# Split weight tiles with longer rows, and pools that begin on multiples of 512 bytes, in a hybrid decoder layer

## The chip, the cores and the metric

One core of one Trainium2 chip runs one layer of a decoder. The metric is device time in microseconds, the median of three runs. A profile of one execution stands beside the times; it also says which clock TensorE was granted.

## What is computed

x has 256 tokens of 2048 channels, all in fp32. The layer is

```
h      = rms_norm(x, mix_norm)
proj   = h @ w_in
mixers = dilated attention, RG-LRU, sliding GQA, SSD   (from slices of proj)
merged = sum over 4 branches of sigmoid(gate_b) * (mixer_b @ w_branch[b])
x      = x + merged @ w_out
gate, up = split(rms_norm(x, ffn_norm) @ w_ffn_in)
x      = x + (silu(gate) * up) @ w_ffn_out
```

The weights are some 354 MB, each used once for the 256 tokens. Most of the work is these five products with big weights.

## The kernel before, in words

**One helper does all the big products.** `stream` (L123 to L156) works off one chunk of at most 512 columns of a weight. For every two row blocks of 128 (one `kg`, KG = 2) it takes a raw fp32 tile `wr`, makes its high part `wh` on ScalarE (a copy into fp32r, L143) and its low part `wl = wr - wh` on VectorE (L145), and multiplies. A tile `wr` comes by one DMA for four row blocks. The product of two fp32 numbers is made of three fp32r passes: activations high by `wh` (L151), high by `wl` (L152), low by `wh` (L153). The stationary operand of each pass is a 128 x 128 slice of the transposed activations (512 bytes in each partition); the moving operand is one row of `wh` or `wl`: 512 columns, 2048 bytes in each partition. For each row block there are two token blocks and three passes, so six matmuls, and twelve for each `kg`. A pass is 128 x 512 wide in all chunks but the first four, which are 384 or 396 wide.

**Buffers.** `wh` and `wl` (pool `wp`, tags `whi` and `wlo`) have four buffers each of [128, 2, 512] fp32r, 4096 bytes in each partition, and lie one behind the other; `wr` has three of 8192 bytes behind them. The stationary operands are `hT_hi`, `hT_lo` (then `x2T_hi`, `x2T_lo` in the same place, pool `actp`), `br_hi`, `br_lo` for the branch projections, `gT_hi`, `gT_lo` for the last product, all on the left side of SBUF, and `mT_hi`, `mT_lo` for the output projection (`ps_o`), on the right side.

**Where they lie modulo 512.** SBUF is handed out from 16512 on (left) and down to 229376 less 32 (right). The pool `const` comes first on the left; with `bsb` it is 4640 + 1536 = 6176 bytes long, so `wp` begins at 22688, which is 160 modulo 512. All buffers behind it are multiples of 512 long, so every row of `wh` and `wl` that is 512 wide, and every slice of `hT`, `x2T`, `br` and `gT`, begins at 160 modulo 512. On the right, `x2` (16384 bytes) begins at 212960, which is 480 modulo 512, and the slices of `mT_hi` and `mT_lo` below it begin at 480 too.

**Order.** All instructions are written out in Python; a scheduler orders them by priority, and the weight stream (DMA, `wh`, `wl`) has the highest. Between the chunks' matmuls small pieces of the mixers are let in by `pump` (transposes and attention matmuls in plain fp32, on the same TensorE queue). The chunks come in this order: 5 of the SSD branch (`ps_ssm`), 3 of the LRU branch (`ps_lru`), 16 of attention (`ps_att`), 16 gate chunks (`ps_g`) with 16 branch projections (`ps_b`) between them, 4 of the output projection (`ps_o`), 22 of the FFN (`ps_fg`, `ps_fu` in turn), 4 of its last product (`ps_fo`).

**The bias vector.** `bias_vector` (L261) runs once, early: one small matmul, a copy into `bsb` (L265) and a DMA to DRAM (L266). `staged` (L322) copies a chunk's results from PSUM into tiles `stg` of the tag `tok`, which has three buffers in the pool `aq`.

Of the kernel before, what the change touches and what calls it, by code (L numbers as in the profile page):

```python
# [18 lines left out]
P = 128  # L19
# [7 lines left out]
KG = 2  # L27
# [8 lines left out]
G0 = M0 + 768 + 1280 + 12  # L36

UNITS = [("c", 0), ("c", 1)] + [("a", h) for h in range(6)]
SSM_W = (384, 384, 384, 396, 512)


def unit_slices():
    """128-column slices of the attention branches: (unit, kind, index, start)."""
    out = []
    for u, (kind, i) in enumerate(UNITS):
        if kind == "c":
            out += [(u, "q", g, C0 + (3 * i + g) * DH) for g in range(3)]
            out += [(u, "k", 0, C0 + 768 + i * DH), (u, "v", 0, C0 + 1024 + i * DH)]
        else:
            out += [(u, s, g, ((si * 3 + g) * 6 + i) * DH) for si, s in enumerate("qkv") for g in range(3)]  # L50
    return out
# [5 lines left out]


def chunk_plan():
    """Column slices (start, width) of w_in in the order in which they are worked off."""  # L60
    z, xbc, dt = M0, M0 + 768, M0 + 768 + 1280
    plan = [("ssm", j, [(xbc + 384 * j, 384)]) for j in range(3)]
    plan += [("ssm", 3, [(xbc + 1152, 128), (z, 256), (dt, 12)]), ("ssm", 4, [(z + 256, 512)])]
    plan += [("lru", j, [(L0 + 512 * j, 512)]) for j in range(3)]
    plan += [("att", j, [(c, DH) for _, _, _, c in SL[4 * j : 4 * j + 4]]) for j in range(len(SL) // 4)]
    return plan


def group_size(kc, first=False):
    """Row blocks of a weight that one transfer carries."""  # L70
    return KG if first or kc % KD else KD


# [1 line left out]
def hybrid(ctx, tc, a):  # L75
    nc = tc.nc
    V, A, G, PE = nc.vector, nc.scalar, nc.gpsimd, nc.tensor

    const = ctx.enter_context(tc.tile_pool(name="const", bufs=1))
    wp = ctx.enter_context(tc.tile_pool(name="wp", bufs=4))  # L80
    actp = ctx.enter_context(tc.tile_pool(name="actp", bufs=1))
    psm = ctx.enter_context(tc.tile_pool(name="psm", bufs=2, space=PSUM))
    psx = ctx.enter_context(tc.tile_pool(name="psx", bufs=4, space=PSUM))
    dram = ctx.enter_context(tc.tile_pool(name="dram", bufs=1, space=DRAM))

    def ctile(shape, name, src=None, dt=F32):
        t = const.tile(shape, dt, name=name, tag=name)
        if src is not None:
            nc.sync.dma_start(t, src)
        return t  # L90
# [1 line left out]
    def mps(name):  # L92
        return psx.tile([P, 512], F32, name=name, tag="mps")

# [1 line left out]
    side = {"near": deque(), "far": deque()}  # L96

    def advance(queue):
# [24 lines left out]
    def stream(src, offset, kc, n, hi, lo, name, before=None, first=False):  # L123
        kd = group_size(kc, first)
        ps = psm.tile([P, T, 512], F32, name=f"ps_{name}", tag="psmain")
        for kg in range(kc // KG):
            if before is not None:
                before(kg)
            with tc.high_priority(offset=4000):
                if kg % (kd // KG) == 0:  # L130
                    if first:
                        raw = xp.tile([P, kd, n], F32, name=f"wr_{name}_{kg}", tag="wfirst", bufs=6)
                    else:
                        raw = wp.tile([P, kd, n], F32, name=f"wr_{name}_{kg}", tag="wraw", bufs=RAW, padded_shape=[P, KD, 512])
                    o = offset + kg * P * KG * n
                    nc.sync.dma_start(
                        raw,
                        bass.AP(tensor=src.tensor, offset=src.offset + o, ap=[[kd * n, P], [n, kd], [1, n]]),
                    )
                q = kg % (kd // KG) * KG  # L140
                rk = raw[:, q : q + KG]
                wh = wp.tile([P, KG, n], F32R, name=f"wh_{name}_{kg}", tag="whi")
                A.activation(wh, rk, AF.Copy)  # L143
                wl = wp.tile([P, KG, n], F32R, name=f"wl_{name}_{kg}", tag="wlo")
                V.tensor_tensor(wl, rk, wh.bitcast(F32), op=ALU.subtract)  # L145
            last = kg == kc // KG - 1
            for kk, t in [(kk, t) for t in range(T) for kk in range(KG)] if last else [(kk, t) for kk in range(KG) for t in range(T)]:
                k = kg * KG + kk
                xh, xl = hi[:, k, t * P : (t + 1) * P], lo[:, k, t * P : (t + 1) * P]
                o_ps = ps[:, t, :n]  # L150
                PE.matmul(o_ps, xh, wh[:, kk], start=(k == 0), stop=False)  # L151
                PE.matmul(o_ps, xh, wl[:, kk], start=False, stop=False)  # L152
                PE.matmul(o_ps, xl, wh[:, kk], start=False, stop=(k == kc - 1))  # L153
            if kg < kc // KG - 1:
                pump()
        return ps  # L156

# [1 line left out]
    with tc.high_priority(offset=4100):  # L159
        gmix = ctile([P, 16], "gmix", a["mix_norm"])  # L160
    actA_hi = actp.tile([P, 16, S], F32R, name="hT_hi", tag="actA_hi")
# [16 lines left out]
    V.memset(negh, -0.5)  # L178

    def rsqrt(out, ss, scale, eps, n):  # L180
        """out = (ss * scale + eps) ** -0.5 on [P, n]"""
        t = const.tile([P, n], F32, name="rsq_t", tag=f"rsq{n}", bufs=2)
        V.tensor_scalar(t, ss, scale, eps, op0=ALU.mult, op1=ALU.add)
        G.tensor_tensor(out, t, negh.to_broadcast([P, n]), op=ALU.pow)
# [37 lines left out]
    ps_first = [next_chunk("ssm", load_input), next_chunk("ssm", load_tokens)]  # L222
    head.close()

# [1 line left out]
    ident = ctile([P, P], "ident", a["ident"])  # L226
    tri = ctile([P, P], "tri", a["tri"])
    ones = ctile([P, P], "ones")
# [22 lines left out]
    V.tensor_scalar(lgb, lgb, 0.5, None, op0=ALU.mult)  # L251
    V.tensor_scalar(snorm, snorm, 0.5, None, op0=ALU.mult)

# [1 line left out]
    tabx = ctile([36, 24], "tabx")  # L255
    nc.sync.dma_start(tabx[0:32, :], a["rel_bias_table"])
    nc.sync.dma_start(tabx[32:36, :], a["group_neg"])
# [3 lines left out]
    def bias_vector():  # L261
        bps = mps("bias_ps")
        PE.matmul(bps[:24, :384], tabx, onehot, start=True, stop=True)
        bsb = ctile([24, 384], "bsb")
        V.tensor_copy(bsb, bps[:24, :384])  # L265
        nc.sync.dma_start(bvec, bsb)  # L266
        yield

    mix = ExitStack()
# [5 lines left out]
        br_lo[b] = pool.tile([P, 6, S], F32R, name=f"br_lo{b}", tag=f"br_lo{b}")  # L275

    def softplus(pool, x, n, name):
        """max(x, 0) + log1p(exp(-|x|)), the logarithm by its series in e / (2 + e)."""

        def st(s):  # L280
            return pool.tile([P, n], F32, name=f"{name}_{s}", tag=f"{name}_{s}", bufs=1)
# [15 lines left out]
        return pl  # L297

    def transpose4(blocks, name):
        """Up to four [128, 128] blocks, transposed into one bank."""  # L300
        ps = mps(name)
        for i, b in enumerate(blocks):
            PE.transpose(ps[:, i * P : (i + 1) * P], b, ident)
        return ps

    # =============== SSD and LRU branches ===============
    branch_operands(3)
    branch_operands(1)
    att1 = ExitStack()
# [10 lines left out]
                V.scalar_tensor_tensor(out[:, b], src[:, b, k : k + S], w[:, b, k : k + 1], out[:, b], op0=ALU.mult, op1=ALU.add)  # L320

    def staged(ps, n, name):  # L322
        """[tokens, n] of PSUM, normalised, as one SBUF tile for each token block."""
        out = []
        for t in range(T):
            stg = aq.tile([P, 512], F32, name=f"stg_{name}{t}", tag="tok", bufs=3)
            A.activation(stg[:, :n], ps[:, t, :n], AF.Copy, scale=r1[:, t : t + 1])
            out.append(stg)
        return out
# [6 lines left out]
            )  # L336
            yield

    # z and dt by token; x, B, C by channel
    zz = sp_.tile([P, T, BW], F32, name="zz", tag="zz")  # L340
    dtx = sp_.tile([P, T, 12], F32, name="dtx", tag="dtx")
    xbcT = sp_.tile([P, 10, S + 3], F32, name="xbcT", tag="xbcT")
# [188 lines left out]
    def lru_body():  # L531
# [40 lines left out]
                    )  # L572

        def decay(s2):
            """a and 1 - a^2 = tanh(-log a) (1 + a^2)"""
            for b in range(s2.start, s2.stop):
                A.activation(th[:, b], tr[:, b], AF.Tanh, scale=c4[:, b : b + 1], bias=c4[:, b : b + 1])
                A.activation(la[:, b], tr[:, b], AF.Exp, scale=nc4[:, b : b + 1], bias=nc4[:, b : b + 1])
# [29 lines left out]
        later(to_channels(staged(ps, 512, f"l{j}"), 4, lruT, 4 * j, f"l{j}"), "near", 1)  # L608
    later(lru_body(), "far", 3)

    # =============== attention branches ===============
    pools = {}
    att = ExitStack()
    unit = [{} for _ in UNITS]
# [12 lines left out]
        return unit[u][s]  # L627

    def qkv_chunk(ps, sl, name):
        """[tokens, slices] in PSUM -> q and k normalised and transposed to [dh, slice, tokens], v by token."""  # L630
        qk = [(i, x) for i, x in enumerate(sl) if x[1] != "v"]
        m = len(qk)
        toks = []
# [143 lines left out]
        later(qkv_chunk(next_chunk("att"), SL[4 * j : 4 * j + 4], f"t{j}"), "near")  # L777
        advance(side["near"])

    # =============== gates, branch projections, merge ===============  # L780
    order = (1, 3, 2, 0)
    gmp = pools["gate"]

# [36 lines left out]
                    G.tensor_tensor(mg[:, t], mg[:, t], gt[:, t], op=ALU.add)  # L820
        later(merged_channels(c, mg), "near", 2)

    # =============== output projection, residual, FFN norm ===============
    x2 = pools["res"].tile([P, T, D], F32, name="x2", tag="x2")
    nc.sync.dma_start(x2, a["x"].rearrange("(t p) d -> p t d", p=P))
    ss2 = ctile([P, T, 4], "ss2")
# [36 lines left out]
    hrr2 = ctile([P, T], "hrr2")  # L863
    V.tensor_tensor(hrr2, hr2, r2, op=ALU.mult)

    # =============== FFN ===============
    def gated_channels(j, sa):
        for q in range(2):
            tp = transpose4([sa[:, t, (2 * q + i) * P : (2 * q + i + 1) * P] for i in range(2) for t in range(T)], f"ftp{j}{q}")
# [28 lines left out]


def _blocks(w, slices, first=False):  # L900
    """[K, n] columns as contiguous [group, partition, k, n] blocks."""
    m = np.concatenate([w[:, o : o + n] for o, n in slices], axis=1)
    k, n = m.shape
    kd = group_size(k // P, first)
    return np.ascontiguousarray(m.reshape(k // P // kd, kd, P, n).transpose(0, 2, 1, 3)).reshape(-1)
# [21 lines left out]


def _cols(v, n):
    """[n*128] -> [128, n]"""  # L930
    return np.ascontiguousarray(np.asarray(v).reshape(n, P).T)


def _layout(i):
# [4 lines left out]
    parts = [_blocks(w_in, sl, (kind, j) == ("ssm", 0)) for kind, j, sl in chunk_plan()]  # L939
    parts += [_blocks(w_in, [(G0 + b * D + c * 512, 512)]) for c in range(4) for b in (1, 3, 2, 0)]  # L940
    onehot, neg = _bias_constants()
    conv = lambda w, b, n: np.ascontiguousarray(  # noqa: E731
        np.concatenate([np.asarray(w)[0], np.asarray(b)[0][None]], 0).reshape(5, n, P).transpose(2, 1, 0)
    )
    qa, qc = np.asarray(i["qk_norm_a"])[0], np.asarray(i["qk_norm_c"])[0]
# [43 lines left out]
```

## Time and profile before

| | |
|---|---|
| median of 3 runs | 1905.21 us (1904.8 to 1905.32) |
| span of the profiled execution (first to last instruction) | 1903.2 us |
| its time outside the span, by the median of the runs | 2.0 us |
| granted TensorE clock, mean | 1.000 of 2.4 GHz |
| PE busy | 1891.0 us (99%), 8714 matmul records |
| PEld (weight loads, beside PE) | 1577.9 us (83%) |
| DVE, ACT, POOL busy | 1081.3, 860.3, 178.5 us |
| DMA | 358.09 MB, mean 188 GB/s |
| chain that ended last | PE 98%, issue 2% |

A matmul's recorded duration runs on beyond the start of the next one, because matmuls are pipelined. What one costs in a row of them is the distance from its start to the next start, which the timeline shows to 10 ns; over a dozen of them the mean is good to 1 ns. The profiled execution's own time is not listed apart from the three runs, so it is taken as its span and the 2.0 us that lie around it.

### The profile page before, as it was taken

The page shows a single profiled execution, that of the slowest core. Times are in us where ns is not written, and L with a number is a line of the kernel's source. Part 1 is how long each engine was busy: PE and PEld are TensorE (multiplying, and loading weights), DVE is VectorE, ACT ScalarE, POOL GpSimd, SP SyncE. Part 2 cuts the span into 40 slices and gives each one's busy share as a digit, 9 for nine tenths or more (in the row PEclk, how much of TensorE's full clock was granted, in tenths as well). Part 3 has the DMA queues.
Part 4 walks back from the last instruction along what each step waited for, and adds up shares of the span by engine and source line. Part 5 has one row for each costly group of instructions (what it writes and reads, how often), then busy time and mean ns, then how long its engine had stood idle before and what let it go on. Part 6 is the DMA issues. An engine that isn't in the chain of part 4 may idle for free.

```text
span 1903.2 us, 21867 instructions
## 1 busy us (share of the span) xinstructions
PE 1891.0 (99%) x8714; PEld 1577.9 (83%) x8714; DVE 1081.3 (57%) x1234; ACT 860.3 (45%) x1052; POOL 178.5 (9%) x152
## 2 busy tenths in 40 slices
PE   8999999999999999999999999999999999999998
PEld 8988888888888888888888888888888888888887
DVE  6867886555555555555555555555555555544443
ACT  6645654444444444444444444444444444433332
POOL 0032322222220000100000100000000000000000
PEclk9999999999999999999999999999999999999999
DMA  8644454454544554555546545555555555555552
GB/s 294 203 154 171 162 210 170 163 185 177 185 171 169 199 213 163 211 186 191 209 166 221 188 177 178 197 181 195 187 190 193 184 198 180 196 187 201 209 209 101
DMA packets 64915, 358.09 MB, mean 188 GB/s; under 512 B 8049, under 2 KB 17581, under 8 KB 26925
## 3 DMA queue, kind: packets, MB, share of 16 engines
q1 hardware_dynamic: 64812, 356.70, 52.6%
q8 instruction: 68, 1.11, 0.2%
q14 instruction: 35, 0.28, 0.0%
HBM read 354.54 MB, written 2.13 MB: 187 GB/s over the span
## 4 chain that ended last, share of the span: by engine, by line
PE 98%; issue 2%; DVE 0%; POOL 0%; DVEq 0%; POOLq 0%
PE ps_att L151 6%; PE ps_att L153 6%; PE ps_att L152 6%; PE ps_g L151 6%; PE ps_g L153 6%; PE ps_g L152 6%; PE ps_fg L153 4%; PE ps_fg L151 4%; PE ps_fg L152 4%; PE ps_fo L151 4%; PE ps_fu L153 4%; PE ps_fu L152 4%; PE ps_fo L152 4%; PE ps_fo L153 4%; PE ps_fu L151 4%; PE ps_b L151 2%
## 5 line engine op out<-in xcount | busy, mean ns | idle before, releaser
L145 DVE TENSOR_TENSOR wl_g<-wr_g,wh_g 128x1024 fp32r<-128x1024 f32 x128 | 170.0, 1328 | 145.7 <-ACT wh_g L143 145.6
L143 ACT ACTIVATE wh_g<-wr_g 128x1024 fp32r<-128x1024 f32 x128 | 135.9, 1062 | 194.2 <-PE ps_g L153 118.6
L145 DVE TENSOR_TENSOR wl_att<-wr_att,wh_att 128x1024 fp32r<-128x1024 f32 x128 | 159.6, 1250 | 92.4 <-ACT wh_att L143 92.2
L143 ACT ACTIVATE wh_att<-wr_att 128x1024 fp32r<-128x1024 f32 x128 | 135.5, 1060 | 163.9 <-PE ps_att L153 145.2
L151 PE MATMUL ps_att<-wh_att,hT_hi 128*128 128x512 f32 x512 | 206.3, 403 | 0.0
L151 PE MATMUL ps_g<-wh_g,hT_hi 128*128 128x512 f32 x512 | 200.5, 392 | 0.0
L153 PE MATMUL ps_att<-wh_att,hT_lo 128*128 128x512 f32 x512 | 199.9, 391 | 0.0
L152 PE MATMUL ps_att<-wl_att,hT_hi 128*128 128x512 f32 x512 | 199.6, 390 | 0.0
L153 PE MATMUL ps_g<-wh_g,hT_lo 128*128 128x512 f32 x512 | 199.3, 389 | 0.0
L152 PE MATMUL ps_g<-wl_g,hT_hi 128*128 128x512 f32 x512 | 199.3, 389 | 0.0
L145 DVE TENSOR_TENSOR wl_fo<-wr_fo,wh_fo 128x1024 fp32r<-128x1024 f32 x88 | 107.9, 1226 | 124.7 <-ACT wh_fo L143 124.7
L145 DVE TENSOR_TENSOR wl_fu<-wr_fu,wh_fu 128x1024 fp32r<-128x1024 f32 x88 | 107.9, 1226 | 118.9 <-ACT wh_fu L143 118.9
L145 DVE TENSOR_TENSOR wl_fg<-wr_fg,wh_fg 128x1024 fp32r<-128x1024 f32 x88 | 107.8, 1225 | 106.9 <-ACT wh_fg L143 106.9
L143 ACT ACTIVATE wh_fo<-wr_fo 128x1024 fp32r<-128x1024 f32 x88 | 93.4, 1061 | 145.9 <-PE ps_fo L153 139.3
L143 ACT ACTIVATE wh_fg<-wr_fg 128x1024 fp32r<-128x1024 f32 x88 | 93.4, 1061 | 143.4 <-PE ps_fg L153 70.3
L143 ACT ACTIVATE wh_fu<-wr_fu 128x1024 fp32r<-128x1024 f32 x88 | 93.4, 1061 | 133.9 <-PE ps_fg L153 72.9
L151 PE MATMUL ps_fg<-wh_fg,x2T_hi 128*128 128x512 f32 x352 | 139.1, 395 | 0.0
L153 PE MATMUL ps_fg<-wh_fg,x2T_lo 128*128 128x512 f32 x352 | 137.3, 390 | 0.0
L151 PE MATMUL ps_fo<-wh_fo,gT_hi 128*128 128x512 f32 x352 | 137.1, 390 | 0.0
L152 PE MATMUL ps_fg<-wl_fg,x2T_hi 128*128 128x512 f32 x352 | 137.1, 389 | 0.0
L153 PE MATMUL ps_fo<-wh_fo,gT_lo 128*128 128x512 f32 x352 | 137.0, 389 | 0.0
L152 PE MATMUL ps_fo<-wl_fo,gT_hi 128*128 128x512 f32 x352 | 136.9, 389 | 0.0
(257 smaller groups left out, 3766.8 us busy)
## 6 DMA issues: line engine op xcount, KB each, us to landing
wr_att<-in_w_in SPq DMA_DIRECT2D x64, 1024.0 KB, 4.7
wr_g<-in_w_in SPq DMA_DIRECT2D x64, 1024.0 KB, 4.8
wr_fg<-in_w_ffn_in SPq DMA_DIRECT2D x44, 1024.0 KB, 4.7
wr_fu<-in_w_ffn_in SPq DMA_DIRECT2D x44, 1024.0 KB, 4.7
wr_fo<-in_w_ffn_out SPq DMA_DIRECT2D x44, 1024.0 KB, 4.8
wr_b<-in_w_branch SPq DMA_DIRECT2D x48, 512.0 KB, 3.5
wr_o<-in_w_out SPq DMA_DIRECT2D x16, 1024.0 KB, 4.8
wr_lru<-in_w_in SPq DMA_DIRECT2D x12, 1024.0 KB, 4.8
```

The source lines that it names most:

```text
L143: A.activation(wh, rk, AF.Copy)
L145: V.tensor_tensor(wl, rk, wh.bitcast(F32), op=ALU.subtract)
L151: PE.matmul(o_ps, xh, wh[:, kk], start=(k == 0), stop=False)
L152: PE.matmul(o_ps, xh, wl[:, kk], start=False, stop=False)
L153: PE.matmul(o_ps, xl, wh[:, kk], start=False, stop=(k == kc - 1))
```

## The change

Each `wh` buffer is allotted rows of 528 elements instead of 512 (2112 bytes), each `wl` buffer rows of 520 (2080 bytes); the columns in use stay the same. The two rows of a tile are then no longer one contiguous run. `wp` moves to the bottom of the left side, `actp` behind it, `const` behind that, with paddings so that the left stack and the right side begin on multiples of 512 (`pad_l` 384 bytes, `pad_r` 480, `pad_c` 480). `bsb` gives up its place in `const` and takes a buffer of the tag `tok`. Comments and docstrings are dropped; those hunks are left out here.

```diff
+LINE = 512
+SB_LOW, SB_TOP = 16512, 212960
+CONST = 4640
...
-    const = ctx.enter_context(tc.tile_pool(name="const", bufs=1))
+
+    def pad(name, n, side="left"):
+        pool = ctx.enter_context(tc.tile_pool(name=name, bufs=1, side=side))
+        pool.tile([P, n // 4], F32, name=name, tag=name)
+
+    pad("pad_l", -SB_LOW % LINE)
+    pad("pad_r", SB_TOP % LINE, "right")
     wp = ctx.enter_context(tc.tile_pool(name="wp", bufs=4))
     actp = ctx.enter_context(tc.tile_pool(name="actp", bufs=1))
+    const = ctx.enter_context(tc.tile_pool(name="const", bufs=1))
+    pad("pad_c", -CONST % LINE)
...
-                wh = wp.tile([P, KG, n], F32R, name=f"wh_{name}_{kg}", tag="whi")
+                wh = wp.tile([P, KG, n], F32R, name=f"wh_{name}_{kg}", tag="whi", padded_shape=[P, KG, 528])
                 A.activation(wh, rk, AF.Copy)
-                wl = wp.tile([P, KG, n], F32R, name=f"wl_{name}_{kg}", tag="wlo")
+                wl = wp.tile([P, KG, n], F32R, name=f"wl_{name}_{kg}", tag="wlo", padded_shape=[P, KG, 520])
                 V.tensor_tensor(wl, rk, wh.bitcast(F32), op=ALU.subtract)
...
-        bsb = ctile([24, 384], "bsb")
-        V.tensor_copy(bsb, bps[:24, :384])
-        nc.sync.dma_start(bvec, bsb)
+        bsb = aq.tile([P, 512], F32, name="bsb", tag="tok", bufs=3)
+        V.tensor_copy(bsb[:24, :384], bps[:24, :384])
+        nc.sync.dma_start(bvec, bsb[:24, :384])
```

Worked out from these sizes, the places modulo 512 become:

| | before | changed |
|---|---|---|
| rows of `wh` (4 buffers x 2 rows) | all 160 | 0, 64, 128, ... 448 |
| rows of `wl` (4 buffers x 2 rows) | all 160 | 0, 32, 64, ... 224 |
| slices of `hT`, `x2T`, `br`, `gT` | 160 | 256 |
| slices of `mT` (`ps_o`) | 480 | 0 |

`wp` begins at 16896 = 33 x 512; four buffers of 4224 bytes end at 33792 = 66 x 512, where `wl` begins; its four buffers of 4160 bytes end at 50432, which is 256 modulo 512, and `wr` and all that follows keep that 256.

The order of TensorE's instructions, of POOL's and of the DMA issues on SP stays the same. On VectorE the splits change their form. In the FFN, before (each `wl` is the low part of a weight, made from `wr` and `wh`; `sa` holds the gated values):

```order
L887 SCALAR_TENSOR_TENSOR sa_10963<-sa_10963,ps_fg_10812 128x512
L145 TENSOR_TENSOR wl_fu_5_11057<-wr_fu_4_11037,wh_fu_5_11055 128x1024
L145 TENSOR_TENSOR wl_fu_6_11075<-wr_fu_6_11071,wh_fu_6_11073 128x1024
L145 TENSOR_TENSOR wl_fu_7_11091<-wr_fu_6_11071,wh_fu_7_11089 128x1024
L145 TENSOR_TENSOR wl_fg_0_11112<-wr_fg_0_11108,wh_fg_0_11110 128x1024
```

and changed:

```order
L898 SCALAR_TENSOR_TENSOR sa_10975<-sa_10975,ps_fg_10824 128x512
L156 TENSOR_TENSOR wl_fu_5_11069<-wr_fu_4_11049,wh_fu_5_11067 128x2x512
L156 TENSOR_TENSOR wl_fu_6_11087<-wr_fu_6_11083,wh_fu_6_11085 128x2x512
L156 TENSOR_TENSOR wl_fu_7_11103<-wr_fu_6_11083,wh_fu_7_11101 128x2x512
L156 TENSOR_TENSOR wl_fg_0_11124<-wr_fg_0_11120,wh_fg_0_11122 128x2x512
```

One run of 1024 elements has become two rows of 512; the order is the same.

On ScalarE, in the fourth SSD chunk, where `bsb` takes a buffer of `stg` (a chunk's results, staged), before:

```order
L143 ACTIVATE wh_ssm_2_727<-wr_ssm_2_725 128x792
L143 ACTIVATE wh_ssm_3_748<-wr_ssm_2_725 128x792
L327 ACTIVATE stg_s_667<-ps_ssm_496,r_83 128x384
L327 ACTIVATE stg_s_669<-ps_ssm_496,r_83 128x384
L143 ACTIVATE wh_ssm_4_771<-wr_ssm_4_769 128x792
L318 ACTIVATE cv<-xbcT,scw 128x256 x3
L143 ACTIVATE wh_ssm_5_801<-wr_ssm_4_769 128x792
```

and changed:

```order
L154 ACTIVATE wh_ssm_2_739<-wr_ssm_2_737 128x2x396
L154 ACTIVATE wh_ssm_3_760<-wr_ssm_2_737 128x2x396
L338 ACTIVATE stg_s_679<-ps_ssm_508,r_95 128x384
L154 ACTIVATE wh_ssm_4_783<-wr_ssm_4_781 128x2x396
L338 ACTIVATE stg_s_681<-ps_ssm_508,r_95 128x384
L329 ACTIVATE cv<-xbcT,scw 128x256 x3
L154 ACTIVATE wh_ssm_5_813<-wr_ssm_4_781 128x2x396
```

The second `stg` now comes behind one weight split. On VectorE a few pieces of the convolution (`cv`, `xbcT`) that hang on it change places with weight splits in the same chunk; that is all that moves.

## Rows read from the trace of the kernel before

**Rows 1.** The page: busy time by engine, TensorE clock in 40 slices, and the last chain.
```profile
PE 1891.0 (99%) x8714; PEld 1577.9 (83%) x8714; DVE 1081.3 (57%) x1234; ACT 860.3 (45%) x1052; POOL 178.5 (9%) x152
...
PEclk9999999999999999999999999999999999999999
...
PE 98%; issue 2%; DVE 0%; POOL 0%; DVEq 0%; POOLq 0%
```

**Rows 2.** What TensorE waited for, all of it: line, releaser, us, times, longest.
```profile
PE ps_ssm L151 <- ACT hT_hi L174: 6.8, 1, 6.8
PE ps_ssm L152 <- DVE wl_ssm L145: 0.5, 1, 0.5
```

**Rows 3.** Whole span, instructions of L151 alone: PE busy (count), PEld busy (count), clock, DMA.
```profile
0.00:1903.20 1903.20, 1042.72 (x2656) 499.57 (x2656) 1.00 0.53 188
```

**Rows 4.** Timeline of PE in `ps_fu`: start us, duration us, line, operands.
```profile
1200.03 0.39 PE L151 MATMUL ps_fu<-wh_fu,x2T_hi 128*128 128x512 f32 x1
...
1202.75 0.39 PE L151 MATMUL ps_fu<-wh_fu,x2T_hi 128*128 128x512 f32 x1
```

**Rows 5.** Timeline of PE in `ps_o`, whose stationary slices lie at 480.
```profile
1092.11 0.39 PE L153 MATMUL ps_o<-wh_o,mT_lo 128*128 128x512 f32 x1
...
1094.91 0.39 PE L153 MATMUL ps_o<-wh_o,mT_lo 128*128 128x512 f32 x1
```

**Rows 6.** Lines by form, `ps_o` against `ps_fu`: count, busy us, mean ns, idle before.
```profile
L151 PE MATMUL ps_fu<-wh_fu,x2T_hi 128*128 128x512 f32 x352 | 136.9, 389 | 0.0
L151 PE MATMUL ps_o<-wh_o,mT_hi 128*128 128x512 f32 x128 | 51.3, 401 | 0.0
L153 PE MATMUL ps_o<-wh_o,mT_lo 128*128 128x512 f32 x128 | 50.6, 396 | 0.0
L152 PE MATMUL ps_o<-wl_o,mT_hi 128*128 128x512 f32 x128 | 50.6, 395 | 0.0
```

**Rows 7.** Timeline of PE in `ps_fg`, behind four transposes, until the next four.
```profile
1215.67 0.60 PE L303 MATMUL ftp<-ident,sa 128*128 128x128 f32 x4
1216.03 0.48 PE L151 MATMUL ps_fg<-wh_fg,x2T_hi 128*128 128x512 f32 x1
1216.34 0.40 PE L152 MATMUL ps_fg<-wl_fg,x2T_hi 128*128 128x512 f32 x1
...
1218.43 0.39 PE L152 MATMUL ps_fg<-wl_fg,x2T_hi 128*128 128x512 f32 x1
1218.65 0.39 PE L153 MATMUL ps_fg<-wh_fg,x2T_lo 128*128 128x512 f32 x1
```

**Rows 8.** The weight splits in `ps_fu`: durations min/median/max in ns.
```profile
L143 ACT ACTIVATE wh_fu<-wr_fu x88: 1060/1061/1062, 1183.3 to 1647.2; 128x1024 fp32r<-128x1024 f32 x88
L145 DVE TENSOR_TENSOR wl_fu<-wr_fu,wh_fu x88: 1224/1226/1227, 1184.4 to 1648.3; 128x1024 fp32r<-128x1024 f32 x88
```

**Rows 9.** Timeline around the bias vector's copy and the second staging.
```profile
61.72 1.17 ACT L327 ACTIVATE stg_s<-ps_ssm,r 128x384 f32<-128x384 f32 x2
61.83 0.55 DVE L265 COPY bsb<-bias_ps 24x384 f32<-24x384 f32 x1 [1.12 <-PE bias_ps L263]
...
62.40 0.30 SPq L266 DMA_DIRECT2D bvec<-bsb  x1
```

## The prediction

> **What bounds the kernel now.** Start with the page [rows 1]: PE is busy for 99% of the span, it holds 98% of the chain that ended last, and its clock stands at full speed in all 40 slices. So neither data, nor another engine, nor the clock is the limit. The waits of PE say the same [rows 2]: 7.3 us in the whole span, all at the start. ACT (45%) and DVE (57%) have room. Time can only change where matmuls follow each other at another distance. A busy PE does not say how fast it goes, so the next view is the timeline, read from start to start.
>
> Lines L151, L152 and L153 have 2656 matmuls each [rows 3], so 3 x 2656 = 7968 fp32r passes. Of these 384 are 384 or 396 columns wide (four chunks of 96); 7584 are 512 wide, 384 of them in `ps_o` (four chunks of 96) and 7200 elsewhere.
>
> Three distances can be seen for the same shape. In `ps_fu` twelve gaps take 1202.75 - 1200.03 = 2.72 us: 226.7 ns each [rows 4]. In `ps_o` twelve gaps take 1094.91 - 1092.11 = 2.80 us: 233.3 ns [rows 5]; its mean durations of 395 to 401 ns stand against 389 in `ps_fu` [rows 6]. In `ps_fg`, behind four transposes, nine gaps take 1218.43 - 1216.34 = 2.09 us: 232.2 ns, and the single ones go up and down between 0.22 and 0.24 before they settle [rows 7]. The 512 columns at one per cycle of 2.4 GHz are 213.3 ns. So a settled matmul carries 226.7 - 213.3 = **13.4 ns** beyond its columns. That it is 20.0 ns in `ps_o`, with the same engine, shape and clock, and with nothing awaited, makes it no constant of the instruction. What differs there is where the stationary slices lie: 480 modulo 512 against 160, with all moving rows at 160. While the columns of one matmul are read (2048 bytes in each partition), the next weight load reads 512 bytes, and it starts with it; the two reads appear to get in each other's way, by an amount that hangs on their places and on the moment. That is my reading; no row shows the reads themselves.
>
> **The change, part by part.**
>
> *Places.* Of the eight `wh` rows one begins where the stationary slice begins (256), seven elsewhere; of the eight `wl` rows none does. No row of the trace shows those relations, so the price of a 512-wide matmul has to be bounded. Below: at best all of the 13.4 ns goes, and the distance is 213.3. Above: the dearest steady distance shown, `ps_o` with 233.3, 6.6 ns more than settled. Neither end is nearer: `ps_o` has other places, but one relation only, and one which the change abolishes (`mT` goes from 480 to 0); the rows of `ps_fg` have equal places, but are out of step in time. So I take the middle: (13.4 - 6.6) / 2 = 3.4 ns saved, a distance of 223.3.
>
> - 7200 matmuls x 3.4 ns = 24.5 us saved.
> - `ps_o`: 384 x (233.3 - 223.3 = 10.0 ns) = 3.8 us saved.
> - the 384 narrow ones: 384 x 3.4 = 1.3 us saved.
>
> Every fp32r matmul stands on the path (the chain is 98% PE), so nothing of this is hidden: 29.6 us.
>
> Here two rules of the Trainium skill speak. "SBUF — State Buffer", section "Who interferes with whom", gives TensorE two independent read ports, one for the moving operand and one for weight loads, and says that only the port shared by VectorE and GpSimd causes contention. By that rule places mean nothing, and the sum would be zero. The 233.3 against 226.7 ns above speaks against it, as far as one relation can. "TensorE: Matmul & The Clock Gate", section "Back-to-back issue gap", gives N / 2.4 + 2.5 ns, 215.8 ns for 512 columns; as an estimate from it, 10.9 ns of the 13.4 could go at most. No row of an fp32r matmul here comes down to that.
>
> *Weight splits.* `wh` and `wl` are written as two rows of 512 and no longer as one run. No row shows this form. It costs nothing at best; at worst a second start for each, which I bound by doubling: 1061 ns on ACT and 1226 ns on DVE [rows 8] would become 2.1 and 2.5 us. Twelve matmuls (12 x 226.7 = 2.72 us) cover a `kg`, and four buffers of each lie ahead, so even that end leaves PE fed in the FFN. I take zero; the cover goes only if DVE's other work in the attention chunks comes on top of a doubled split. This end adds at most some us to the upper side.
>
> *bsb.* It holds one of three `tok` buffers from its copy at 61.83 until the DMA issued at 62.40 has been read [rows 9]; the second `stg` waits for it, one weight split later. Behind it on ACT stand pieces of the convolution and the next splits. Bounds: nothing, or the few us of a small DMA, once. What covers it: the staged chunk's PSUM tile is wanted only a chunk later, 96 matmuls of this stage on. If it is not covered, 1 to 3 us. I take zero. The paddings and the move of `const` cost no instruction, no DMA and no wait.
>
> *Sum.* Against the profiled execution: span 1903.2 + 2.0 around it = 1905.2, the median of the runs to 0.1 us. 1905.2 - 29.6 = **1875.6, say 1876 us**. What the measurement can tell from no change is about 0.2%, 3.8 us.
>
> **The rivals.**
>
> 1. *The settled step is lost* (slower). With all rows at one place, the matmuls fall into step: the gaps settle from 232 on average to 226.7, and stay so until small matmuls break in [rows 4, 7]. After the change the place of the moving row differs with each matmul, `wh` against `wl` and buffer against buffer. If the step needs equal places, it is never found, and all matmuls run as behind the transposes: 7200 x (232.2 - 226.7 = 5.5 ns) = 39.6 us, 2.1 us for the narrow ones, 0.4 us gained in `ps_o`; less some 6 us, since a part of the 7200 already runs unsettled behind interruptions. About +35 us: **1940 us**. It decides from the point where the mean distance passes 226.7 + 0.5 ns (0.5 x 7584 = 3.8 us). For it: the only other relation shown is dearer, and the gaps of the unsettled stretch lie mostly above 226.7. Against it: those gaps belong to equal places, and some of them are already below.
>
> 2. *Places decide nothing for the moving rows* (no change). Then the step is set by the stationary slice or by time alone, and only `ps_o` may fall to the common distance: 384 x 6.6 = 2.5 us. **1903 us.** The rule on independent ports, above, leads here too. Against it stands again `ps_o`.
>
> 3. *Most of the excess goes*: with the two reads mostly apart, two thirds of 13.4 ns are saved: 7200 x 8.9 + 384 x 15.5 + 384 x 8.9 = 73 us, **1832 us**. Against it: nothing in fp32r passes comes near that distance in the trace.
>
> 4. *The rows are merged back, and the change does not do what it says.* The order above excludes it: the splits have become 2x512.
>
> **How the numbers follow.** My forecast, some of the excess goes, from 1852 to 1898: 0.38. Rival 3 and what lies between it and the forecast, below 1852: 0.10. Rival 2, within 3.8 us of 1905: 0.15. Rival 1, from 1910 up to 1955 (the dearest single gaps of 236 ns for all would be 1975): 0.37. So faster 0.48, same 0.15, slower 0.37. The sign is nearly open, because the trace has one relation of places beside the equal one; I lean to faster because the settled excess of 13.4 ns leaves twice as much to win as `ps_o` shows to lose. The range holds 8 in 10: it gives up the fastest cases below 1848 (0.09) and the dearest above 1946 (0.11). The likeliest case alone is 1852 to 1898.
>
> **What would show it.** In `ps_fu` twelve gaps would take 2.68 us or less where they now take 2.72; rival 1 shows 2.78 or more and no settling, with gaps that differ from matmul to matmul; rival 2 shows 2.72 and a repeated step. In `ps_o` twelve gaps should fall from 2.80. The splits should keep about 1061 and 1226 ns, and PE's waits their 7.3 us at the start; a wait on `wh` or `wl` later on would mean that the second row has a price after all. A wait of `stg` on the bias vector's DMA is expected, and none of PE behind it. I am wrong if the mean distance of 512-wide matmuls rises, or if it falls while the time does not.

## The result, and the profile after

The changed kernel takes 1935.95 us (median of 4 runs, 1935.6 to 1936.34) against 1905.09 us (4 runs, 1904.8 to 1905.32): a ratio of 1.016, 95% interval 1.0148 to 1.0172. It is **slower by 1.6%, 30.9 us**. The forecast was 1876 us.

The page of the changed kernel, first the busy times, then the granted clock in 40 slices and the last chain:

```profile
PE 1922.2 (99%) x8714; PEld 1579.4 (82%) x8714; DVE 1081.8 (56%) x1234; ACT 860.2 (44%) x1052; POOL 177.8 (9%) x152
...
PEclk9999999999999999999999999999999999999999
...
PE 99%; DMA 0%; DVE 0%; SPq 0%; ACT 0%; DVEq 0%; issue 0%
```

And all that PE waited for (line, releaser, us, times, longest):

```profile
PE ps_ssm L162 <- ACT hT_hi L185: 7.3, 1, 7.3
```

Beside [rows 1, 2] nothing has changed but PE's own busy time: 1891.0 to 1922.2 us, 31.2 more, with as many matmuls, a granted clock of 0.999 of 2.4 GHz on the mean (1.000 before), and no new wait. VectorE, ScalarE and GpSimd have the same work. The time went into the distance from matmul to matmul.

The timeline of PE in `ps_fu` of the changed kernel (start us, duration us, line, operands) answers to [rows 4]:

```profile
1209.72 0.40 PE L162 MATMUL ps_fu<-wh_fu,x2T_hi 128*128 128x512 f32 x1
1209.96 0.39 PE L163 MATMUL ps_fu<-wl_fu,x2T_hi 128*128 128x512 f32 x1
1210.19 0.39 PE L164 MATMUL ps_fu<-wh_fu,x2T_lo 128*128 128x512 f32 x1
1210.42 0.39 PE L162 MATMUL ps_fu<-wh_fu,x2T_hi 128*128 128x512 f32 x1
1210.64 0.40 PE L163 MATMUL ps_fu<-wl_fu,x2T_hi 128*128 128x512 f32 x1
1210.88 0.39 PE L164 MATMUL ps_fu<-wh_fu,x2T_lo 128*128 128x512 f32 x1
...
1212.50 0.39 PE L162 MATMUL ps_fu<-wh_fu,x2T_hi 128*128 128x512 f32 x1
```

Twelve gaps take 2.78 us, 231.7 ns each, where 2.72 us stood before. The single ones are 0.24, 0.23, 0.23, 0.22, 0.24: they go on like those of [rows 7] behind the transposes, and do not settle. The end of `ps_o` answers to [rows 5]:

```profile
1182.68 0.39 PE L163 MATMUL ps_o<-wl_o,mT_hi 128*128 128x512 f32 x1
...
1185.00 0.39 PE L164 MATMUL ps_o<-wh_o,mT_lo 128*128 128x512 f32 x1
```

Ten gaps, 2.32 us: 232.0 ns, a little below the 233.3 of before. The lines by form (count, busy us, mean ns, idle before) bring the two stages nearer to each other, where [rows 6] had 389 and 401 ns:

```profile
L162 PE MATMUL ps_fu<-wh_fu,x2T_hi 128*128 128x512 f32 x352 | 138.5, 394 | 0.0
...
L162 PE MATMUL ps_o<-wh_o,mT_hi 128*128 128x512 f32 x128 | 51.1, 399 | 0.0
```

**The account.** Taken over all starts in the two traces: 6976 gaps between successive 512-wide fp32r matmuls outside `ps_o` (without the first gap behind each interruption) sum to 1584.9 us before and 1615.7 after, a mean of 227.2 against 231.6 ns: +30.8 us. `ps_o`, the gaps behind interruptions left in, goes from 88.4 to 87.7: -0.6. The 384 narrow ones go from 71.1 to 71.4: +0.3. The first matmul starts 0.5 us later (its wait on `hT_hi` is 7.3 us where it was 6.8), and the gaps next to interruptions bring another 0.3. Together that is 31.3 us, the difference of the two spans (1934.5 - 1903.2).

The weight splits of the changed kernel (min/median/max ns) answer to [rows 8]:

```profile
L154 ACT ACTIVATE wh_fu<-wr_fu x88: 1059/1060/1062, 1200.2 to 1673.1; 128x1024 fp32r<-128x1024 f32 x88
...
L156 DVE TENSOR_TENSOR wl_fu<-wr_fu,wh_fu x88: 1224/1226/1229, 1201.3 to 1674.2; 128x1024 fp32r<-128x1024 f32 x88
```

Two rows of 512 cost what one run of 1024 cost. And ScalarE's timeline where `bsb` takes a buffer of `tok` ([rows 9] before):

```profile
63.07 0.58 ACT L338 ACTIVATE stg_s<-ps_ssm,r 128x384 f32<-128x384 f32 x1 [0.49 <-PE tch_s L314]
...
65.11 0.87 ACT L154 ACTIVATE wh_ssm<-wr_ssm 128x792 fp32r<-128x792 f32 x1 [1.45 <-PE ps_ssm L164]
...
65.88 0.56 ACT L338 ACTIVATE stg_s<-ps_ssm,r 128x384 f32<-128x384 f32 x1
```

The second `stg` starts 2.81 us after the first, behind one split, where both stood together before. The wait of `stg` on the bias vector's DMA, which the prediction expected, does not show as idle time of ScalarE, and PE has no wait that comes of it.

### The profile page after: what moved, and what is told of

It is laid out like the page before. It is cut to its first block, busy times and chain, and to the rows that moved or that the text cites. A ratio compares the mean times of both kernels' runs of the same rounds, so it can differ in the third digit from the quotient of the medians.

```text
span 1934.5 us, 21867 instructions
## 1 busy us (share of the span) xinstructions
PE 1922.2 (99%) x8714; PEld 1579.4 (82%) x8714; DVE 1081.8 (56%) x1234; ACT 860.2 (44%) x1052; POOL 177.8 (9%) x152
## 4 chain that ended last, share of the span: by engine, by line
PE 99%; DMA 0%; DVE 0%; SPq 0%; ACT 0%; DVEq 0%; issue 0%
PE ps_g L163 6%; PE ps_att L162 6%; PE ps_g L162 6%; PE ps_g L164 6%; PE ps_att L163 6%; PE ps_att L164 6%; PE ps_fg L163 4%; PE ps_fo L163 4%; PE ps_fu L163 4%; PE ps_fu L162 4%; PE ps_fo L164 4%; PE ps_fo L162 4%; PE ps_fg L162 4%; PE ps_fu L164 4%; PE ps_fg L164 4%; PE ps_b L164 2%
## 5 line engine op out<-in xcount | busy, mean ns | idle before, releaser
L154 ACT ACTIVATE wh_att<-wr_att 128x1024 fp32r<-128x1024 f32 x128 | 135.4, 1060 | 169.8 <-PE ps_att L164 150.2
L156 DVE TENSOR_TENSOR wl_fo<-wr_fo,wh_fo 128x1024 fp32r<-128x1024 f32 x88 | 107.8, 1226 | 129.5 <-ACT wh_fo L154 129.5
L156 DVE TENSOR_TENSOR wl_fu<-wr_fu,wh_fu 128x1024 fp32r<-128x1024 f32 x88 | 107.9, 1226 | 124.2 <-ACT wh_fu L154 124.2
L154 ACT ACTIVATE wh_fo<-wr_fo 128x1024 fp32r<-128x1024 f32 x88 | 93.3, 1060 | 151.1 <-PE ps_fo L164 144.3
L154 ACT ACTIVATE wh_fu<-wr_fu 128x1024 fp32r<-128x1024 f32 x88 | 93.3, 1060 | 139.2 <-PE ps_fg L164 75.7
L162 PE MATMUL ps_fu<-wh_fu,x2T_hi 128*128 128x512 f32 x352 | 138.5, 394 | 0.0
L163 PE MATMUL ps_fu<-wl_fu,x2T_hi 128*128 128x512 f32 x352 | 138.5, 394 | 0.0
```

## The experiments

All of them compute the whole layer. "Place" is the start of a row or slice modulo 512 bytes; "relation" is the place of the stationary slice minus that of the moving row, modulo 256 unless said otherwise. "Steady distance" is the mean from start to start over all the traced starts of `ps_fu` (moving rows against `x2T`), and over those of `ps_o` (against `mT`) that lie more than twelve gaps behind an interruption. The expectations of experiments 3 and 4 count a relation the other way round, moving minus stationary modulo 512: their 192 and 448 are both 64 here. The kernel before, run beside them, took 1906.72 us (first four), 1905.89 (next four) and 1905.41 (median of 15, last three). The times of experiments 1 to 10 are of one run each; differences below some 2 us are not read from them.

**1. Plain rows, everything else as changed.** Against the changed kernel:

```diff
-                wh = wp.tile([P, KG, n], F32R, name=f"wh_{name}_{kg}", tag="whi", padded_shape=[P, KG, 528])
+                wh = wp.tile([P, KG, n], F32R, name=f"wh_{name}_{kg}", tag="whi", padded_shape=[P, KG, 512])
...
-                wl = wp.tile([P, KG, n], F32R, name=f"wl_{name}_{kg}", tag="wlo", padded_shape=[P, KG, 520])
+                wl = wp.tile([P, KG, n], F32R, name=f"wl_{name}_{kg}", tag="wlo", padded_shape=[P, KG, 512])
```

All moving rows, and the slices of `hT`, `x2T`, `br`, `gT` and `mT`, then lie at 0.

> The changed kernel with plain rows of 2048 bytes again; the pools stay on multiples of 512, so all moving rows, all stationary slices and mT lie at 0 modulo 512. Theory A (the settled step needs moving rows that all begin at the same place; rows at many places lose it): 226.7 ns in ps_fu, and in ps_o too if equal places are all it needs; 1902 to 1905 us. Theory B (each pair of places, moving minus stationary, has its own price, and the changed kernel pays the mean of many): relation 0 as before, 226.7 ns, 1902 us; in this kernel A and B agree. Theory C (the move of the pools, not the rows, is what costs): 231 to 232 ns stays, 1936 us.

Measured: 1902.43 us. PE's busy time, then its timeline in `ps_fu` and `ps_fg`, and in `ps_o`:

```profile
PE 1888.1 (99%) x8714; PEld 1577.3 (83%) x8714; DVE 1079.2 (57%) x1234; ACT 859.8 (45%) x1052; POOL 179.5 (9%) x152
...
1209.77 0.39 PE L162 MATMUL ps_fu<-wh_fu,x2T_hi 128*128 128x512 f32 x1
...
1212.49 0.39 PE L162 MATMUL ps_fg<-wh_fg,x2T_hi 128*128 128x512 f32 x1
...
1119.85 0.39 PE L162 MATMUL ps_o<-wh_o,mT_hi 128*128 128x512 f32 x1
...
1122.57 0.39 PE L162 MATMUL ps_o<-wh_o,mT_hi 128*128 128x512 f32 x1
```

Twelve gaps take 2.72 us in both stages: 226.7 ns. With the longer rows taken away the loss is gone, with the moved pools, the paddings and `bsb` in `tok` all kept. And `ps_o`, 233.3 ns before, runs like the others once its slices lie where the rows lie.

**2. The longer rows alone**, in the kernel before:

```diff
-                wh = wp.tile([P, KG, n], F32R, name=f"wh_{name}_{kg}", tag="whi")
+                wh = wp.tile([P, KG, n], F32R, name=f"wh_{name}_{kg}", tag="whi", padded_shape=[P, KG, 528])
...
-                wl = wp.tile([P, KG, n], F32R, name=f"wl_{name}_{kg}", tag="wlo")
+                wl = wp.tile([P, KG, n], F32R, name=f"wl_{name}_{kg}", tag="wlo", padded_shape=[P, KG, 520])
```

> The kernel before with the longer rows (2112 and 2080 bytes) alone; no padding, const and bsb where they were. Theory A: the step is lost as in the changed kernel, about 231.6 ns in ps_fu and ps_o, 1936 us. Theory B: other relations than in the changed kernel (moving rows at 32 to 480, stationary at 416), so another mean, anywhere from 224 to 236 ns. Theory C: 226.7 ns, 1905 us.

Measured: 1936.29 us, as the whole change. The timeline in `ps_fu` gives 2.77 us for twelve gaps:

```profile
1209.98 0.39 PE L152 MATMUL ps_fu<-wl_fu,x2T_hi 128*128 128x512 f32 x1
...
1212.75 0.39 PE L152 MATMUL ps_fu<-wl_fu,x2T_hi 128*128 128x512 f32 x1
```

So two lines of the diff carry the whole loss. Here the wandering rows have other places than in the changed kernel (the `wh` rows 32, 96, ... 480, the slices 416), and the mean is the same.

**3 and 4. All moving rows at one place, the slices at another.** Against experiment 1, the first puts `x2T` and its like at 256 and `mT` at 64, the second at 128 and 320:

```diff
-    pad("pad_r", 480, "right")
+    pad("pad_r", 416, "right")
...
+    pad("pad_x", 256)
     actp = ctx.enter_context(tc.tile_pool(name="actp", bufs=1))
```

(480 is what `SB_TOP % LINE` gives; the second has 160 and 128 for 416 and 256).

> As e1 (all moving rows at 0), but stationary slices at 256 and mT at 64 modulo 512. Theory A: equal moving places are all that counts, 226.7 ns in ps_fu and ps_o. Theory B: relations 256 and 448 have prices of their own; 256 was 231.6 on average over wh rows in the changed kernel, so about 231 in ps_fu and anything in ps_o.

> As e1 (all moving rows at 0), but stationary slices at 128 and mT at 320 modulo 512, which is the relation 192 that ps_o had before. Theory A: 226.7 ns in ps_fu and ps_o. Theory B: ps_o at 233.3 ns as before; ps_fu (relation 384) at a price of its own, 232.3 if the mean of that relation in the changed kernel carries over.

Measured: 1905.47 and 1942.26 us. Experiment 3, `ps_fu`, and then `ps_o`:

```profile
1210.12 0.39 PE L163 MATMUL ps_fu<-wh_fu,x2T_hi 128*128 128x512 f32 x1
...
1212.61 0.39 PE L165 MATMUL ps_fu<-wh_fu,x2T_lo 128*128 128x512 f32 x1
...
1119.66 0.39 PE L163 MATMUL ps_o<-wh_o,mT_hi 128*128 128x512 f32 x1
...
1122.46 0.39 PE L163 MATMUL ps_o<-wh_o,mT_hi 128*128 128x512 f32 x1
```

Eleven gaps of `ps_fu`, 2.49 us: 226.4, the settled step, with the slices 256 away. Twelve of `ps_o`, 2.80 us: 233.3. Neither theory had both: A missed `ps_o`, and B missed `ps_fu`. Experiment 4, `ps_fg` into `ps_fu`:

```profile
1209.80 0.39 PE L163 MATMUL ps_fg<-wh_fg,x2T_hi 128*128 128x512 f32 x1
...
1212.59 0.39 PE L163 MATMUL ps_fu<-wh_fu,x2T_hi 128*128 128x512 f32 x1
```

Twelve gaps, 2.79 us: 232.5 ns with the slices 128 away, and the whole kernel is slower than the changed one. Rows at one place are therefore not enough; the slices count as well. And 256 counts as nothing.

**5. Longer rows again, but by 256 bytes.** Against the changed kernel, `wh` has rows of 576 elements (2304 bytes) and `wl` plain ones; the rows then alternate between the places 128 and 384, which is one place modulo 256, and all slices have it too:

```diff
-    pad("pad_l", -SB_LOW % LINE)
-    pad("pad_r", SB_TOP % LINE, "right")
+    pad("pad_r", 96, "right")
...
-    pad("pad_c", -CONST % LINE)
+    pad("pad_c", -CONST % 256)
...
-                wh = wp.tile([P, KG, n], F32R, name=f"wh_{name}_{kg}", tag="whi", padded_shape=[P, KG, 528])
+                wh = wp.tile([P, KG, n], F32R, name=f"wh_{name}_{kg}", tag="whi", padded_shape=[P, KG, 576])
...
-                wl = wp.tile([P, KG, n], F32R, name=f"wl_{name}_{kg}", tag="wlo", padded_shape=[P, KG, 520])
+                wl = wp.tile([P, KG, n], F32R, name=f"wl_{name}_{kg}", tag="wlo", padded_shape=[P, KG, 512])
```

> wh rows longer by 256 bytes (2304), wl rows plain; wh rows then lie at 128 and 384 modulo 512, wl at 128, all stationary slices at 128 or 384: all equal modulo 256, two places modulo 512. Theory D (formed after e1 to e4: the settled step needs every moving row and every stationary slice to agree modulo 256; any other place costs 5 to 7 ns): 226.7 ns in ps_fu and ps_o, 1902 to 1904 us. Theory A (any difference among the moving rows loses the step): 231 ns or more, about 1935 us.

Measured: 1903.16 us. The timeline from `ps_fu` into `ps_fg`:

```profile
1209.81 0.39 PE L161 MATMUL ps_fu<-wh_fu,x2T_hi 128*128 128x512 f32 x1
...
1212.53 0.39 PE L161 MATMUL ps_fg<-wh_fg,x2T_hi 128*128 128x512 f32 x1
```

Twelve gaps, 2.72 us. Rows of `wh` that differ modulo 512, that are longer, and whose splits are written in two rows are all there, and the step is kept. This is the run on which the theory that any difference among the rows loses the step falls; what is left is the place modulo 256.

**6 and 7. One of the two tiles.** Of the changed kernel the first leaves only `wl` with longer rows, the second only `wh`. The edits are one line each:

```diff
-                wh = wp.tile([P, KG, n], F32R, name=f"wh_{name}_{kg}", tag="whi", padded_shape=[P, KG, 528])
+                wh = wp.tile([P, KG, n], F32R, name=f"wh_{name}_{kg}", tag="whi", padded_shape=[P, KG, 512])
```

```diff
-                wl = wp.tile([P, KG, n], F32R, name=f"wl_{name}_{kg}", tag="wlo", padded_shape=[P, KG, 520])
+                wl = wp.tile([P, KG, n], F32R, name=f"wl_{name}_{kg}", tag="wlo", padded_shape=[P, KG, 512])
```

In both the plain rows and all slices have one place modulo 256.

> The changed kernel with the longer rows of wl alone (2080 bytes); wh rows plain, at 0; one pass in three then has a moving row off the common place. Theory D with a step that is lost by any row off place: 230 to 232 ns on all three passes, 1925 to 1936 us. If each row paid for itself (rival): a third of the loss, 226.7 + 1.6 = 228.3 ns, about 1914 us.

> The changed kernel with the longer rows of wh alone (2112 bytes); wl rows plain, at 0; two passes in three have a moving row off the common place, except in one buffer of four (rows at 0 and 256 modulo 512 come in two of the eight places). Theory D: 230 to 232 ns, 1925 to 1936 us. If each row paid for itself: two thirds of the loss, 229.9 ns, about 1925 us.

Measured: 1938.22 and 1933.65 us; the first is 2.2 us above the range it was given. In experiment 7 two of the eight `wh` rows, at 0 and 256, lie right too, each in a buffer with one that does not. Lines by form of experiment 6, the three passes of `ps_fu` (count, busy us, mean ns, idle before):

```profile
L162 PE MATMUL ps_fu<-wh_fu,x2T_hi 128*128 128x512 f32 x352 | 139.2, 395 | 0.0
L163 PE MATMUL ps_fu<-wl_fu,x2T_hi 128*128 128x512 f32 x352 | 139.1, 395 | 0.0
L164 PE MATMUL ps_fu<-wh_fu,x2T_lo 128*128 128x512 f32 x352 | 138.2, 393 | 0.0
```

and of experiment 7:

```profile
L164 PE MATMUL ps_fu<-wh_fu,x2T_lo 128*128 128x512 f32 x352 | 138.5, 394 | 0.0
L162 PE MATMUL ps_fu<-wh_fu,x2T_hi 128*128 128x512 f32 x352 | 138.5, 394 | 0.0
L163 PE MATMUL ps_fu<-wl_fu,x2T_hi 128*128 128x512 f32 x352 | 138.2, 393 | 0.0
```

No pass is at the 389 ns of the settled step [rows 6]. Sorted by the place of the moving row, from start to start: in experiment 6 the `wh` passes with the slices' own place (two passes in three) are 231.5 ns apart, in experiment 7 the `wl` passes with it 230.9. Here the idea that each row pays for its own place falls: it would have spared two thirds of the loss in the one and a third in the other. One pass in three off its place costs all three. The changed kernel shows the same: its `wh` rows at 0 and 256 and its `wl` row at 0 have the slices' place modulo 256, and in `ps_fu` they are followed by gaps of 230.5, 231.7 and 230.8 ns on the mean, where the sixteen rows lie between 229.5 and 234.2. None is near 226.7.

**8, 9 and 10. Three more relations**, each with all moving rows at 0; the edit is that of experiments 3 and 4 with other numbers:

```diff
-    pad("pad_r", 480, "right")
+    pad("pad_r", 448, "right")
...
+    pad("pad_x", 192)
     actp = ctx.enter_context(tc.tile_pool(name="actp", bufs=1))
```

The second has 320 and 96; the third 224 and no `pad_r`. So `mT` lies at 32, 160 and 480.

> As e1 (plain rows, all at 0), stationary slices at 192, mT at 32 modulo 512. Theory D: 232 to 234 ns in both ps_fu and ps_o, about 1945 us. Rival (moving rows equal among themselves settle at some step of their own, different for each place, and one may be lower than 226.7): ps_fu or ps_o below 226 ns.

> As e1 (plain rows, all at 0), stationary slices at 96, mT at 160 modulo 512. Theory D as mended after e8 (only the place modulo 256 counts, 0 is the cheapest, every other one has a steady price of its own between 228 and 234 ns): ps_fu and ps_o each within 228 to 234 ns, 1910 to 1950 us. Rival (some place is cheaper than equal places): below 226 ns in one of them.

> As e1 (plain rows, all at 0), stationary slices at 224, mT at 480 modulo 512, which is the same place modulo 256. Theory D: ps_fu and ps_o at one and the same distance to 0.2 ns, within 228 to 234 ns. If the place modulo 512 counts: the two differ. Rival: below 226 ns.

Measured: 1919.3, 1955.2 and 1947.36 us. The timelines of `ps_fu` (192) and of `ps_fg` (96, then 224), the first two with `ps_o` behind (32 and 160):

```profile
1209.87 0.39 PE L163 MATMUL ps_fu<-wh_fu,x2T_hi 128*128 128x512 f32 x1
...
1212.61 0.39 PE L163 MATMUL ps_fu<-wh_fu,x2T_hi 128*128 128x512 f32 x1
...
1121.06 0.40 PE L163 MATMUL ps_o<-wh_o,mT_hi 128*128 128x512 f32 x1
...
1123.86 0.40 PE L163 MATMUL ps_o<-wh_o,mT_hi 128*128 128x512 f32 x1
```

```profile
1209.98 0.39 PE L163 MATMUL ps_fg<-wh_fg,x2T_hi 128*128 128x512 f32 x1
...
1212.79 0.40 PE L163 MATMUL ps_fg<-wh_fg,x2T_hi 128*128 128x512 f32 x1
...
1121.02 0.39 PE L163 MATMUL ps_o<-wh_o,mT_hi 128*128 128x512 f32 x1
...
1123.82 0.39 PE L163 MATMUL ps_o<-wh_o,mT_hi 128*128 128x512 f32 x1
```

```profile
1209.78 0.39 PE L163 MATMUL ps_fg<-wl_fg,x2T_hi 128*128 128x512 f32 x1
...
1212.58 0.39 PE L163 MATMUL ps_fg<-wl_fg,x2T_hi 128*128 128x512 f32 x1
```

Twelve gaps take 2.74, 2.81 and 2.80 us, and 2.80 in both of the `ps_o`. Experiment 8 missed its expectation in `ps_fu` (228.9 and not 232 to 234 ns), and 9 lies just above its range (234.3 ns, 1955.2 us); in 10 the two stages agree, and no distance is below 226. With `ps_o` of these runs all eight multiples of 32 have been seen, every moving row at one place:

| relation modulo 256 | steady distance, ns | seen in |
|---|---|---|
| 0 | 226.7 | before, 1, 3 (256 apart), 5 |
| 32 | 233.3 | `ps_o` of 8 |
| 64 | 233.3 | `ps_o` of before, of 3, of 4 |
| 96 | 234.3 | 9 |
| 128 | 232.4 | 4 |
| 160 | 233.3 | `ps_o` of 9 |
| 192 | 228.9 | 8 |
| 224 | 233.3 | 10, `ps_o` of 10 |
| rows of mixed places | 231.3 to 231.9 | changed, 2, 6, 7 |

Relation 0 is the best of the eight. If each matmul paid the price of its own row by this table, the changed kernel would stand at 230.9 ns, experiment 6 at 228.4 and 7 at 229.1; they stand at 231.6, 231.9 and 231.3. That the mixtures lie near the mean of the eight, 231.9, is therefore no explanation of them.

The traces also show two kinds of dear distance. Where all moving rows have one place and the slices another, the gaps repeat: in `ps_fu`, to 1 ns and through all eleven of its chunks, every third gap has the same length in experiment 8, every fourth in 10, and every seventh in 4 and 9. Those matmuls do settle, as the rival of experiment 8 had it, but into a pattern that is dearer on the mean, not cheaper. Where the rows have mixed places (changed, 2, 6, 7), nothing repeats: for no n up to 48, after which the same buffers come round, are more than 41% of the gaps as long, to 1 ns, as the gap n before.

**11. Experiment 1 once more**, in rounds against the kernel before.

> e1 again, timed: plain rows, everything at 0 modulo 512. Against the kernel before only ps_o's 384 matmuls change, from 233.3 to about 227 ns: 2.4 us less, ratio 0.9987. Theory D and theory A agree on it; the rival that the paddings or the buffer of bsb cost something would leave 1905 us or more.

Measured: 1902.49 us (median of 11, 1901.45 to 1904.37) against 1905.41: a ratio of 0.9986, 95% interval 0.9977 to 0.9995. It **beats both kernels**, by 2.9 and 33 us. In the trace `ps_o` sums to 86.2 us where it was 88.4; that is 2.2 us of the 2.9.

## Why the prediction was wrong

**The step that failed** is the price of a 512-wide matmul, "So I take the middle: (13.4 - 6.6) / 2 = 3.4 ns saved, a distance of 223.3". The runs show 231.6 in its place, 4.9 ns dearer than the settled step and not 3.4 cheaper. Two things were wrong in it. Its lower end, 213.3 ns, supposed that the whole 13.4 ns beyond the columns come of two reads in each other's way and could go. No run showed any of it going on the mean: at the best relation of eight there are still 226.7. And its sentence "Neither end is nearer" set aside the two rows that stood near. `ps_o` with 233.3 [rows 5] and the unsettled stretch with 232.2 [rows 7] both lay above the settled step, and no steady distance lay below it. The objection to the unsettled stretch, that its places are equal and it is only out of step in time, did not make it a worse guide: the changed kernel runs whole stages with gaps that go up and down like those, at 231.6 on the mean.

**Rival 1 was right**, in mechanism and nearly in price: 1940 us against 1935.95. Its condition was "If the step needs equal places, it is never found". Experiments 3 to 7 make it exact, for the places tried: the step needs every moving row, in all three passes, at the place of the stationary slices modulo 256 bytes. (The prediction compared places modulo 512 and found one row of sixteen that agrees with its slices; modulo 256 three do, and it did not help them.) Its terms: 5.5 ns each for the 512-wide (measured 4.4 on the mean, with the gaps that had been unsettled before in it, so 30.8 us for its 39.6 less 6), 2.1 us for the narrow (0.3), 0.4 us back in `ps_o` (0.6).

**What bounds the kernel** was read rightly: PE alone, by its distances, and that the busy share says nothing of how fast. The whole loss stands on the path.

**`ps_o`** was to fall and fell, from 233.3 to about 232, though by far less than the 10.0 ns forecast. The reading that its excess comes of places is now shown: in experiment 1, with `mT` moved to the rows' place, it is 226.7. Experiments 3 and 4 bring the 233.3 back with the relation of before, 64.

**Places as such.** The prediction weighed a rule of the Trainium skill, "SBUF — State Buffer", section "Who interferes with whom": TensorE's read ports for the moving operand and for weight loads are independent. By it, rival 2 should have come. The runs disagree: with only places changed (experiments 1 and 9), the distance goes from 226.7 to 234.3 ns and the kernel from 1902 to 1955 us. The other page, "TensorE: Matmul & The Clock Gate", section "Back-to-back issue gap", gives 215.8 ns for 512 columns. No steady distance of the fp32r matmuls here, each with a weight load of its own, is below 226.7.

**Splits, `bsb`, pools at nothing**: right. The splits kept 1060 and 1226 ns, PE got no wait, and experiments 1 and 2 divide the change cleanly: without the longer rows no loss, with them alone all of it.

**The numbers.** The time lies in the range only because rival 1 had stretched that to 1946; the forecast itself, 1852 to 1898, does not hold it. The chances leaned to the wrong side, 0.48 to 0.37, on the ground that "the settled excess of 13.4 ns leaves twice as much to win as `ps_o` shows to lose". How much could be won if a stall went is no evidence that it will go.

**What stays open.** The traces show that the two operands' places decide, and modulo what; they do not show the reads. Three questions were not answered: whether the weight load hinders the columns or the columns the weight load, why 192 costs so little, and why rows of mixed places spoil even the passes whose rows lie right.

## What to carry to other kernels

Before a layout is varied, read from the timeline whether the matmuls run at a settled step, and treat it as something that can be lost: in this kernel it held only while all moving rows and all stationary slices began at the same place modulo 256 bytes, and one pass in three off it spoilt all three. Rows that have to be longer kept the step when they were longer by 256 bytes (experiment 5; no other multiple was tried), and a stage with a dearer distance than its like (`ps_o` here) should have its operands' places compared first. Where a cost is bounded from both sides, take the row of the trace that lies nearest in kind, not the middle to a limit that no row has reached.

## What the runs showed of the hardware that was not expected

With equal places the settled distances are whole steps of 16 cycles at 2.4 GHz (granted clock 1.000 in experiment 1). In its trace, timeline of PE, 384 columns wide and then 396:

```profile
29.73 0.33 PE L162 MATMUL ps_ssm<-wh_ssm,hT_hi 128*128 128x384 f32 x1
...
35.97 0.33 PE L162 MATMUL ps_ssm<-wh_ssm,hT_hi 128*128 128x384 f32 x1
...
64.41 0.34 PE L163 MATMUL ps_ssm<-wl_ssm,hT_hi 128*128 128x396 f32 x1
...
68.37 0.34 PE L164 MATMUL ps_ssm<-wh_ssm,hT_lo 128*128 128x396 f32 x1
```

36 gaps in 6.24 us are 173.3 ns, 416 cycles; 22 gaps in 3.96 us are 180.0 ns, 432 cycles; and 226.7 ns are 544. That is 32 cycles beyond 384 and 512 columns, and 36 beyond 396, which is no multiple of 16. With unlike places it is the repeated pattern that is a whole number of such steps: in `ps_fu` three gaps of experiment 8 are 1648 cycles, four of 10 are 2240, seven of 4 are 3904 and seven of 9 are 3936. So some 32 cycles, 13.3 ns, go with every one of these matmuls even at the best places, and none of these runs bears out the prediction's reading of its 13.4 ns as reads in each other's way.

The penalty is not monotonic in the relation either: 192 costs 2.2 ns and its neighbours 160 and 224 cost 6.7 and 6.6. And with equal places the matmuls find their step again by themselves: in the trace of the kernel before, within ten gaps behind an interruption where that many follow. With rows of mixed places they do not find it in the 96 matmuls of a chunk.
